# Weight split in a hybrid decoder block: the low part by ScalarE and an accumulating DMA instead of a VectorE subtraction

## The chip, the core and the metric

The kernel runs on one core of a Trainium2 chip. The metric is device microseconds (us) of one execution, lower is better. In the profile the engines are PE (TensorE matmul) with PEld (its weight load), DVE (VectorE), ACT (ScalarE), POOL (GpSimd) and SP (SyncE, which here only issues DMAs).

## The reference

One block of a decoder over 512 tokens of width 1024, with 16 learned meta tokens put ahead (528 columns in all), everything in float32:

```python
h = concat([meta, x])
h = h + 0.5 * swiglu(rmsnorm(h, ffn1_norm), ffn1_w1, ffn1_w3, ffn1_w2)     # D_FF = 2816
hn = rmsnorm(h, mix_norm)
q, k, v, u, g_attn, g_ssm = split(hn @ w_in)
attn = sliding_window_attention(q, k, v, attn_sinks)   # 16 query heads, 4 key heads of 64, window 128
y = gelu(s5_ssm(u, ...))                               # complex diagonal state space layer, 32 groups of 16 channels
ssm = (y @ ssm_glu_a) * sigmoid(y @ ssm_glu_b)
h = h + (sigmoid(g_attn) * attn + sigmoid(g_ssm) * ssm) @ w_out
h = h + 0.5 * swiglu(rmsnorm(h, ffn2_norm), ffn2_w1, ffn2_w3, ffn2_w2)
return rmsnorm(h, final_norm)[meta tokens dropped]
```

with `swiglu(h, w1, w3, w2) = (silu(h @ w1) * (h @ w3)) @ w2`.

## The kernel before

Every product with a weight matrix is made from three products in the format float32r: both operands are split into a high part (the value rounded to float32r) and a low part (the value minus its high part), and `hi*hi + hi*lo + lo*hi` is accumulated in PSUM. Activations stand with the model dimension on the partitions, tokens on the free axis, and a weight tile is [128, nk, 128]: nk blocks of 128 rows of the weight matrix and 128 of its columns.

**The weight stream.** The weights are cut into 200 pieces, in the order in which they are used. `load_raw` (L146) loads one raw tile by a DMA of SP, of mostly 256 columns, so two pieces; two raw buffers are there. `prep_piece` (L160) makes one piece from its raw tile: ScalarE copies it to the tile `whi` (L173, a rounding to float32r), and VectorE subtracts, `wlo = raw - whi` (L174). `whi` and `wlo` have three buffers each. When the last piece of a raw tile is made, the next raw load is issued. The last 8 pieces go to the columns of two larger tiles of their own (`tails`, seen as `hgh` and `hgl`), and so wait for no buffer.

**The units.** A unit is one output block of 128 rows. It takes one piece (`take`, L183), runs 3 * nk matmuls (twice as many, of 264 columns, where the 528 columns are in use; the order for each block k is hi*hi, hi*lo, lo*hi, L234), and is evacuated by VectorE and ScalarE. `step` (L192) emits the matmuls of unit i, then prepares a piece, then emits the evacuation of unit i. Since three pieces exist before unit 2, the piece made behind the matmuls of unit i is that of unit i+2, and its buffers come free when unit i-1 has ended. Every engine runs its instructions in the order in which they are emitted (the schedule is written out by hand), and the framework adds the waits on semaphores.

**The stages**, with the units of each: the first SwiGLU (44 up units with `p` L238, 32 down units at L412, in chunks of 4, 6, 6 and 6 blocks of 128); projections u, k, v and the first of q (10 units), with the state space layer between their matmuls; the mixed stage, 30 units (`MIX`, L25: q, gates, GLU), with the attention of 16 blocks emitted at 11 cuts in each unit, where `prep_piece` is at cut 8 (`CUT`, L41); the output projection (8 units), whose residual `hT` comes back from DRAM by two DMAs of POOL (L1315); the second SwiGLU (44 up units, 24 down units at L414); and the last chunk's down projection by halves of the tokens (16 units at L1372) with the final norm.

**POOL's own work** stands in POOL's one queue: the parameters of the state space layer during the first SwiGLU (`ssm_params`, L472: one chunk at the middle of each unit, L852), the sums of squares for the norms (`sqs`, L835 and L837), and in the mixed stage the normalised probabilities `E` (L1168), the masked meta probabilities `m4` (L1200) and the low part of the queries `qs` (L1130). DMAs issued from POOL are L479 to L496, L666, L869 and L1315.

Of the kernel before, what the change touches and what calls it, by code (L numbers as in the profile page):

```python
# [10 lines left out]
AF = mybir.ActivationFunctionType  # L11
ALU = mybir.AluOpType
# [48 lines left out]
def fr(ap):  # L61
    return ap.bitcast(F32)
# [3 lines left out]
def hybrid_block_kernel(  # L66
# [30 lines left out]
    V, S, G, PE, SY = nc.vector, nc.scalar, nc.gpsimd, nc.tensor, nc.sync  # L97
# [18 lines left out]

# [1 line left out]
    ident = const.tile([128, 128], F32, name="ident")  # L118
    ones = const.tile([128, 128], F32, name="ones")
# [6 lines left out]

# [1 line left out]
    raws = []  # L128
# [31 lines left out]
    def prep_piece():  # L160
        i = nxt["piece"]
        if i >= len(pieces):
            return
        nxt["piece"] += 1
        r, sl, last, dest = pieces[i]
        src = raw_tiles[r][:, :, sl]
        nk = src.shape[1]
        if dest is None:
            hi = w_p.tile([128, nk, 128], F32R, tag="whi", name="whi")
            lo = w_p.tile([128, nk, 128], F32R, tag="wlo", name="wlo")  # L170
        else:
            hi, lo = tails[0][:, dest], tails[1][:, dest]
        S.activation(out=hi, in_=src, func=AF.Copy)  # L173
        V.tensor_tensor(out=lo, in0=src, in1=fr(hi), op=ALU.subtract)  # L174
        wtiles[i] = (hi, lo)
        if last:
            del raw_tiles[r]
            load_raw()

    state = {"unit": 0}  # L180
# [20 lines left out]
    def step2(ua, ub, mids=()):  # L201
        """Two units of which the last tile of operands comes late: it goes last in both."""
        a, b = ua[0](*take(), None), ub[0](*take(), None)
        next(a)
        for m in mids:
            m()
        prep_piece()
        next(b)
        for g in (a, b):
            for _ in g:  # L210
                pass
        ua[1]()
        prep_piece()
        ub[1]()
# [8 lines left out]
    def accumulate(seq, emit, mids):  # L223
        """One accumulation group; the callables in mids go out between its matmuls."""
        cuts = {len(seq) * (j + 1) // (len(mids) + 1): m for j, m in enumerate(mids)}
        for n, args in enumerate(seq):
            if n in cuts:
                cuts[n]()
            emit(*args, n == 0, n == len(seq) - 1)
# [26 lines left out]

# [1 line left out]
    def ffn_plan(w1, w3, w2, chunks, head=0, tail=False):  # L258
# [43 lines left out]

# [1 line left out]
    def new_hg(cols=COLS, p=hg_p):  # L304
# [44 lines left out]

# [1 line left out]
    def ffn_units(hg, hT, n528, mm_ps, g_p, t_p, chunks, last_hook=None, first_mm=None, tail=False):  # L351
        """The units of one half-residual SwiGLU, hT += 0.5 * its output; with tail, the last chunk's
        down projection is left out and its operands are returned."""
        w = HALF if n528 else 256
# [96 lines left out]

# [1 line left out]
    persist = ExitStack()  # L453
# [18 lines left out]
    def ssm_params(ps_p):  # L472
# [113 lines left out]
        V.tensor_copy(dT, ps[:16, 256:288])  # L586
        # the even groups' rows stay on the lower partitions, the odd ones' on the upper
        for i, (dst, q) in enumerate(((c8[:, 0, :], 2), (c8[:, 1, :], 3), (m8, 4))):
# [106 lines left out]

# [1 line left out]
    G.memset(ones, 1.0)  # L697
# [34 lines left out]
    S.activation(out=rcol[:, 0:1], in_=mhalf[:, 0:1], func=AF.Silu)  # L732
    # the tensor engine's clock rises while the first loads are under way
    ps = ax_ps.tile([128, 512], F32, tag="ax", name="ps_w")
# [26 lines left out]
    def x_in(h, d):  # L761
        """Block columns d of token half h: the transpose, then the two parts one and two blocks later."""
        if d < ND:
            x_t(h, d)
        if 0 <= d - 1 < ND:
            x_hi(h, d - 1)
        if 0 <= d - 2 < ND:
            x_lo(h, d - 2)
# [8 lines left out]
    def first_mm(p, hi, lo, mids):  # L777
        """The first two units take the first half of the tokens first, while the second is brought in."""
        firsts.append((p, hi, lo))
# [86 lines left out]

# [1 line left out]
    hd = tc.dram_tile([128, ND, COLS], F32, name="h_keep")  # L868
# [28 lines left out]
    def ev_u(b):  # L897
        """Step-major u: [channel, (step, chunk)], the two chunks of meta tokens first; by way of DRAM
        it comes back as [(7 - step, channel of the group), (group, chunk)]."""
        def f(p):  # L900
            t = s_p.tile([128, T, NCH], F32, tag="uT", name="uT", bufs=2)

            def steps(v, n):
                return v.rearrange("p h (k s) -> p h k s", s=T) if n else v
            for c0, c1, o in ((0, 256, t[:, :, 2:NCH].rearrange("p s (h k) -> p h k s", h=2)),
                              (256, 264, t[:, :, 0:2].rearrange("p s h -> p h s"))):
                V.tensor_tensor(out=o, in0=steps(p[:, :, c0:c1], c0 == 0), in1=steps(rbv[:, :, c0:c1], c0 == 0), op=ALU.mult)
            SY.dma_start(out=ud[b], in_=t)
        return f
# [146 lines left out]

# [1 line left out]
    ps1.close()  # L1058
# [25 lines left out]
    vmeta(0)  # L1084
    # masks, with the sign that the negated scores need
    for t, m0, p0 in ((mA, 0, 16), (mC, 128, 0)):
# [4 lines left out]
                        pattern=[[-1, 128]], channel_multiplier=1)  # L1091
    # hm[p, h]: 1 where row p of the stacked meta probabilities belongs to head h
    V.tensor_reduce(out=hm, in_=ident.rearrange("p (l h k) -> p h l k", l=2, h=4), axis=mybir.AxisListType.XY, op=ALU.add)
# [77 lines left out]
    def s2(n, c, kb):  # L1171
        """One block of keys: the probabilities' transpose."""
        E, _, tiles = att[n][:3]
# [133 lines left out]

# [1 line left out]
    at.close()  # L1309
# [50 lines left out]

    # the last chunk's down projection by halves of the tokens, each half's norm behind the products
    ps5 = ExitStack()
# [114 lines left out]
```

## Time and profile before

| | |
|---|---|
| Median of the timed runs | 1161.17 us (two runs, 1161.1 and 1161.25) |
| Span of the profiled execution, first to last instruction | 1160.7 us |
| Busy: PE / PEld | 1141.6 us (98%) / 1016.8 us (88%) |
| Busy: DVE / ACT / POOL | 632.1 us (54%) / 410.4 us (35%) / 361.5 us (31%) |
| DMA traffic | 108.42 MB, 93 GB/s on average |

The span leaves out what lies around the instructions: the timed runs are 0.4 to 0.6 us longer. A matmul's end is modelled and matmuls overlap, so the duration of one (0.28 to 0.39 us) is more than the distance from one to the next. A row of the profile with "<-" names output and input tiles; a row that ends in "idle before <-releaser" says how long the engine sat idle and what ended that. The chain of work that ended last is followed back from the last instruction.

### The profile page before, as it was taken

What the parts mean: (1) busy time and instruction counts of PE and PEld (TensorE: products, weight loads), DVE (VectorE), ACT (ScalarE), POOL (GpSimd) and SP (SyncE); (2) the same over time, 40 slices, a digit from 0 to 9 for tenths busy, and PEclk for the clock granted to TensorE, in tenths of its full rate; (3) what the DMA queues carried; (4) which work ended last, traced back from release to release, by engine and by line L of the source; (5) the groups of instructions that cost most, each with busy time, mean ns of one, the idle gap of its engine ahead of it and who ended that gap; (6) DMA issues with size and microseconds to landing.
All of it is one profiled execution on the core that took longest, in us unless ns stands there. A gap on an engine that the chain in (4) does not pass through costs nothing.

```text
span 1160.7 us, 17253 instructions
## 1 busy us (share of the span) xinstructions
PE 1141.6 (98%) x7022; PEld 1016.8 (88%) x7022; DVE 632.1 (54%) x956; ACT 410.4 (35%) x719; POOL 361.5 (31%) x488
## 2 busy tenths in 40 slices
PE   9999999999999999999999999999999999999997
PEld 7999999999999999987778778878888888888887
DVE  5446653645444363767776777564544444444454
ACT  5322232232222242446565464353322222232234
POOL 1966662543685030425454331021000000000003
PEclk7999999999999999999999999999999999999999
DMA  5533233322423246121122222432333223323221
GB/s 158 115 96 109 73 92 94 91 84 83 110 74 101 69 144 191 48 73 60 51 73 73 73 68 79 145 109 73 108 109 110 73 82 103 112 86 117 84 73 73
DMA packets 105582, 108.42 MB, mean 93 GB/s; under 512 B 7504, under 2 KB 101968, under 8 KB 105376
## 3 DMA queue, kind: packets, MB, share of 16 engines
q1 hardware_dynamic: 103104, 100.74, 27.8%
q0 software_dynamic: 2352, 6.52, 2.2%
q8 instruction: 55, 0.90, 0.3%
q14 instruction: 23, 0.19, 0.1%
q10 hardware_dynamic: 48, 0.07, 0.0%
HBM read 100.80 MB, written 5.34 MB: 91 GB/s over the span
## 4 chain that ended last, share of the span: by engine, by line
PE 88%; DVE 4%; ACT 3%; POOL 2%; issue 2%; DMA 1%; POOLq 0%; DVEq 0%; SPq 0%; ACTq 0%
PE p L238 58%; PE p L412 11%; PE p L414 8%; PE p L798 2%; PE p L1372 1%; DMA hT<-h_keep 1%; ACT E L1157 1%; POOL m L1200 1%; POOL E L1168 1%; PE psK L656 1%; PE psY L992 1%; DVE wlo L174 1%; PE ps_x L744 1%; PE psY L993 1%; PE psS L943 1%
## 5 line engine op out<-in xcount | busy, mean ns | idle before, releaser
L238 PE MATMUL p<-hgh,whi 128*128 128x264 f32 (+1 forms) x1408 | 403.4, 333 | 0.1
L238 PE MATMUL p<-hgl,whi 128*128 128x264 f32 (+1 forms) x1408 | 402.4, 332 | 0.0
L238 PE MATMUL p<-hgh,wlo 128*128 128x264 f32 (+1 forms) x1408 | 400.9, 331 | 0.5 <-DVE wlo L174 0.5
L174 DVE TENSOR_TENSOR wlo<-raw,whi 128x1024 fp32r<-128x1024 f32 (+2 forms) x192 | 254.0, 1323 | 104.5 <-ACT whi L173 102.2
L238 PEld LDWEIGHTS p<-hgh,whi 128*128 128x128 f32 x1408 | 238.5, 188 | 26.0 <-issue 1.5
L238 PEld LDWEIGHTS p<-hgh,wlo 128*128 128x128 f32 x1408 | 238.2, 188 | 24.6 <-DVE wlo L174 1.0
L238 PEld LDWEIGHTS p<-hgl,whi 128*128 128x128 f32 x1408 | 238.4, 188 | 22.4
L173 ACT ACTIVATE whi<-raw 128x1024 fp32r<-128x1024 f32 (+2 forms) x192 | 187.5, 979 | 133.1 <-PE p L414 72.2
L1388 POOL TENSOR_TENSOR acc<-acc,zq 128x256 f32<-128x256 f32 x12 | 8.9, 738 | 349.8 <-ACT zq L1381 349.7
L384 ACT ACTIVATE t<-t 128x528 f32<-128x528 f32 (+1 forms) x44 | 28.1, 639 | 164.3 <-DVE t L383 164.3
L394 ACT ACTIVATE gh<-t 128x528 fp32r<-128x528 f32 (+1 forms) x44 | 28.1, 639 | 159.2 <-DVE t L393 159.2
L432 DVE SCALAR_TENSOR_TENSOR hT<-p,hT 128x528 f32<-128x528 f32 (+1 forms) x56 | 39.1, 698 | 82.8 <-PE p L414 52.2
L412 PE MATMUL p<-gh,whi 128*128 128x264 f32 x352 | 72.8, 288 | 0.7 <-DVE hT L432 0.5
L412 PE MATMUL p<-gl,whi 128*128 128x264 f32 x352 | 71.5, 284 | 0.0
L412 PE MATMUL p<-gh,wlo 128*128 128x264 f32 x352 | 71.4, 284 | 0.0
L383 DVE TENSOR_TENSOR t<-p,r_bc 128x528 f32<-128x528 f32 (+1 forms) x44 | 30.7, 698 | 70.4 <-PE p L238 67.3
L393 DVE TENSOR_TENSOR t<-p,t 128x528 f32<-128x528 f32 (+1 forms) x44 | 30.7, 698 | 63.8 <-PE p L238 63.5
L412 PEld LDWEIGHTS p<-gh,whi 128*128 128x128 f32 x352 | 54.4, 188 | 2.3 <-issue 1.2
L414 PE MATMUL p<-gh,whi 128*128 128x512 f32 x144 | 56.0, 389 | 0.0
L414 PE MATMUL p<-gl,whi 128*128 128x512 f32 x144 | 56.0, 389 | 0.0
L414 PE MATMUL p<-gh,wlo 128*128 128x512 f32 x144 | 56.0, 389 | 0.0
L412 PEld LDWEIGHTS p<-gl,whi 128*128 128x128 f32 x352 | 54.6, 188 | 0.0
(322 smaller groups left out, 1516.1 us busy)
## 6 DMA issues: line engine op xcount, KB each, us to landing
raw<-in_ffn_w_dram SPq DMA_DIRECT2D x42, 1024.0 KB, 5.4
raw<-in_ffn_w_dram SPq DMA_DIRECT2D x24, 768.0 KB, 4.3
raw<-in_w_in_dram SPq DMA_DIRECT2D x16, 1024.0 KB, 5.5
raw<-in_ffn_w_dram SPq DMA_DIRECT2D x12, 512.0 KB, 3.5
raw<-in_w_out_dram SPq DMA_DIRECT2D x4, 1024.0 KB, 8.7
h_keep<-hT POOLq DMA_DIRECT2D x1, 2112.0 KB, 7.3
raw<-in_ssm_glu_a_dram SPq DMA_DIRECT2D x4, 512.0 KB, 3.6
raw<-in_ssm_glu_b_dram SPq DMA_DIRECT2D x4, 512.0 KB, 4.6
```

The costliest lines, as they stand in the source:

```text
L173: S.activation(out=hi, in_=src, func=AF.Copy)
L174: V.tensor_tensor(out=lo, in0=src, in1=fr(hi), op=ALU.subtract)
L238: PE.matmul(out=o, lhsT=w[:, k0 + k, :], rhs=sl(r, k), start=start, stop=stop)
L383: V.tensor_tensor(out=t1, in0=cell[1], in1=rb(), op=ALU.mult)
L384: S.activation(out=t1, in_=t1, func=AF.Silu)
L393: V.tensor_tensor(out=t3, in0=cell[3], in1=cell["t1"], op=ALU.mult)
L394: S.activation(out=gh, in_=t3, func=AF.Copy)
L412: PE.matmul(out=p[:, h, :HALF], lhsT=wt[:, k, :], rhs=gs[k][c][:, h, :], start=start, stop=stop)
L414: PE.matmul(out=p, lhsT=wt[:, k, :], rhs=gs[k][c].rearrange("p h c -> p (h c)"), start=start, stop=stop)
L432: V.scalar_tensor_tensor(out=hv(hT, d), in0=cell["p"], scalar=0.5, in1=hv(hT, d), op0=ALU.mult, op1=ALU.add)
L656: PE.matmul(out=ps[:16, 128 * i:128 * i + 128], lhsT=BB[:, 0, g, :], rhs=Qt[:, g, 0:T, :].rearrange("p t c -> p (t c)"), start=True, stop= ...
L798: PE.matmul(out=p[:, h, :HALF], lhsT=w[:, k, :], rhs=r[:, k, h * HALF:(h + 1) * HALF], start=(n == 0), stop=(n == 3 * ND - 1))
```

## The change

The subtraction on VectorE goes. ScalarE writes the negated high part into the `lo` tile, and a DMA from POOL reads the same columns of the weight matrix from DRAM a second time and adds them to what the tile holds. A raw tile that has two sources (GLU) takes two such DMAs for a piece. Beside this, comments and docstrings are dropped, which gives no instruction.

```diff
         S.activation(out=hi, in_=src, func=AF.Copy)
-        V.tensor_tensor(out=lo, in0=src, in1=fr(hi), op=ALU.subtract)
+
+        S.activation(out=lo, in_=fr(hi), func=AF.Copy, scale=-1.0)
+        k0 = 0
+        for s in raws[r][2]:
+            n = s.shape[1]
+            G.dma_start(out=lo[:, k0:k0 + n, :], in_=s[:, :, sl], accum_op=ALU.add)
+            k0 += n
         wtiles[i] = (hi, lo)
         if last:
             del raw_tiles[r]
             load_raw()
```

`S` is ScalarE, `V` VectorE, `G` GpSimd. `s[:, :, sl]` takes 128 columns of float32 of each row of the weight matrix, 512 bytes in one piece, nk rows for each of the 128 partitions.

## The prediction

> **What bounds the kernel now.** I read the head of the page first, then the groups, the chain in order of time, the DMA issues, and short stretches of the timeline.
>
> ```profile
> span 1160.7 us, 17253 instructions
> PE 1141.6 (98%) x7022; PEld 1016.8 (88%) x7022; DVE 632.1 (54%) x956; ACT 410.4 (35%) x719; POOL 361.5 (31%) x488
> ...
> PE 88%; DVE 4%; ACT 3%; POOL 2%; issue 2%; DMA 1%; POOLq 0%; DVEq 0%; SPq 0%; ACTq 0%
> ...
> L238 PE MATMUL p<-hgh,wlo 128*128 128x264 f32 (+1 forms) x1408 | 400.9, 331 | 0.5 <-DVE wlo L174 0.5
> L174 DVE TENSOR_TENSOR wlo<-raw,whi 128x1024 fp32r<-128x1024 f32 (+2 forms) x192 | 254.0, 1323 | 104.5 <-ACT whi L173 102.2
> ...
> L173 ACT ACTIVATE whi<-raw 128x1024 fp32r<-128x1024 f32 (+2 forms) x192 | 187.5, 979 | 133.1 <-PE p L414 72.2
> ```
>
> TensorE is busy 98% of the span and makes 88% of the chain. The matmuls that read `wlo` waited 0.5 us for it in the whole run. So the 254.0 us of VectorE that the change takes away lie beside matmuls, and the 19 us in which PE is idle bound any gain: 1.6%, under the 2% that a measurement of this kernel can tell from no change. What can move the time is how late the low part becomes ready. For that the length of a unit counts, from the chain:
>
> ```profile
> 91.27 3.12 PE p L412 x24
> ...
> 155.27 5.87 PE p L238 x48
> ...
> 301.17 4.41 PE p L412 x36
> ...
> 797.68 54.44 PE p L238 x240
> 852.12 32.64 PE p L414 x144
> ```
>
> An up unit takes 5.87 us in the first SwiGLU and 54.44 / 10 = 5.44 in the second; a down unit of six blocks 4.41 and 32.64 / 8 = 4.08, one of four blocks 3.1. The mixed stage, 30 units:
>
> ```profile
> 512.00:718.00 206.00, 198.05 (x977) 160.28 (x976) 154.03 (x350) 118.87 (x284) 87.65 (x57) 1.00 0.21 67
> ```
>
> That is 6.87 us a unit.
>
> **The change part by part.** Removed: 200 subtractions, of no price on PE but for the waits above and a few places named below. Added on ScalarE: a second copy as long as the first, 0.98 us on average, 200 of them, 196 us more on an engine that is busy 410.4. In the mixed stage ScalarE goes from 118.9 to about 150 of 206 us while VectorE loses 1.3 a unit; I count these against each other, at nothing, covered by matmuls; without that cover it is 30 times 1 us at most. Added on POOL: 208 DMA issues (two of half the size for each of the 8 GLU pieces). Added for DRAM: another 100 MB in rows of 512 bytes. The price is T, from the issue to the landing of an accumulating DMA of 512 KB, and no row shows one. The nearest rows:
>
> ```profile
> raw<-in_ffn_w_dram SPq DMA_DIRECT2D x42, 1024.0 KB, 5.4
> ...
> raw<-in_ssm_glu_a_dram SPq DMA_DIRECT2D x4, 512.0 KB, 3.6
> ...
> are<-in_ssm_a_re_dram POOLq DMA_DIRECT2D x1, 8.0 KB, 1.9
> ...
> q1 hardware_dynamic: 103104, 100.74, 27.8%
> q0 software_dynamic: 2352, 6.52, 2.2%
> ...
> DMA to landing us min/median/max: 7.6/9.3/11.0
> ...
> 740.99 0.99 POOL L1315 DMA_DIRECT2D hT<-h_keep  x1 [21.24 <-PE p L238]
> ```
>
> The lowest end is a plain 512 KB, 3.6 us. The highest: POOL's queue q0 took 0.022 * 16 * 1160.7 / 2352 = 174 ns a packet; 1024 rows on 16 engines at one packet a row are 64 * 0.174 = 11.1, with 1.9 of a tiny POOL DMA 13.0 us. Nearest in kind are the two loads of `hT` (the 7.6/9.3/11.0 row): issued by POOL, 128 partitions of 8 rows as here, 1 KB a row, and an accumulation has to bring 512 bytes from DRAM and 512 from the tile for each row. I take 7.6, the one that landed first, and 11.0 where two raw loads of 1 MB are under way. POOL's issue, 0.99 us, is in it.
>
> The Trainium skill, "DMA: Bandwidth & Descriptors", section "Anatomy of one DMA", fits a POOL DMA as 2.0 us plus its bytes at 436 per ns. That would make 3.2 us here, and the sum below would be that of the first rival; for the 1 MB of `hT` it gives 4.4, and the trace, with other transfers beside it, has 7.6. Against the change speaks "Collectives: The Full Stack", section "The bandwidth ceiling": an add in the DMA path is slow because it needs two source reads, not because of the add. With twice the bytes the fit gives 4.4 us for our DMA; no run here shows it yet.
>
> Now the lookahead. The piece for unit i+2 is made when unit i-1 ends. In the second SwiGLU:
>
> ```profile
> 1107.84 0.69 DVE L383 TENSOR_TENSOR t<-p,r_bc 128x512 f32<-128x512 f32 x1 [1.87 <-PE p L238]
> 1108.56 0.63 ACT L384 ACTIVATE t<-t 128x512 f32<-128x512 f32 x1 [3.85 <-DVE t L383]
> ...
> 1109.10 1.04 ACT L173 ACTIVATE whi<-raw 128x1024 fp32r<-128x1024 f32 x1
> ...
> 1110.18 1.23 DVE L174 TENSOR_TENSOR wlo<-raw,whi 128x1024 fp32r<-128x1024 f32 x1 [0.25 <-ACT whi L173]
> ```
>
> The unit has ended by 1107.84, the high part is there at 1110.14, and the negated copy would be at 1111.2, 3.4 us after the end. The first use is the third matmul of unit i+2, 2 * 5.44 + 0.47 later than the end. T is hidden up to 10.88 + 0.47 - 3.4 = 7.9 us; the first SwiGLU has 2 * 5.87 + 0.5 - 3.7 = 8.5. Down units have smaller tiles (T of 6.2 for six blocks, 4.75 for four, from 1.9 plus the share of 5.7) and no ScalarE evacuation: 2 * 4.08 + 0.5 - 1.8 = 6.9 and 2 * 3.1 + 0.4 - 1.3 = 5.3. So at 7.6 the steady SwiGLUs lose nothing. But each four up units load two raw tiles of 1 MB together: at 11.0 us some 3 us are missing, at 22 such places; I take half of them, 30 us. With the DVE subtraction none of this mattered, since it ended 3.6 us after the unit.
>
> In the mixed stage the piece is made late:
>
> ```profile
> 608.87 1.06 ACT L173 ACTIVATE whi<-raw 128x1024 fp32r<-128x1024 f32 x1
> ...
> 608.99 0.39 PE L238 MATMUL p<-YH,whi 128*128 128x512 f32 x1
> ...
> 610.29 2.02 POOL L1200 TENSOR_TENSOR m<-ms,hm 128x512 fp32r<-128x512 f32 x1
> ```
>
> Unit i ends at 608.99, where the next one's first matmul stands. The DMA is queued behind `m4` on POOL, to 612.3, 3.3 us later, and only unit i+1 lies ahead of its use. From the first use in unit i, 0.5 us into it, two periods hold 6.4 + 3.3 + T: the period is (9.7 + T) / 2 = 8.65 us against 6.87. For 16 units with attention that is 29 us. A unit without has no `m4`: with cut 8 at 4.1 us of 5.6 and 2.1 of ScalarE, (5.7 + T) / 2 = 6.65, 1.05 too much; half of it for 14 units is 7. Sum 36. What is queued behind a DMA on POOL there are `E`, `m4` and `qs` of the next unit, for which PE's transposes wait; they come a DMA issue (1 us) later, inside the same stall.
>
> Single places:
>
> ```profile
> 10.12 1.22 DVE L174 TENSOR_TENSOR wlo<-raw,whi 128x1024 fp32r<-128x1024 f32 x1 [0.52 <-ACT whi L173]
> ...
> 13.98 0.64 PE L798 MATMUL p<-hgh,wlo 128*128 128x264 f32 x2
> ...
> 742.55 11.04 DMA hT<-h_keep
> ...
> 756.72 1.24 DVE wlo L174
> 758.00 31.12 PE p L238 x136
> ...
> 1132.45 0.88 DVE hgl L174
> 1134.54 1.43 PE p L1372 x12
> ...
> L509 POOL TENSOR_TENSOR mag<-e,x 32x64 f32<-32x64 f32 x1 | 11.1, 11126 | 0.0
> L642 POOL TENSOR_TENSOR Qt<-Qt,tq 128x1152 f32<-128x1152 f32 x4 | 13.4, 3345 | 0.3
> ```
>
> Start: copy, negated copy and DMA end at 10.1 + 1.0 + 7.6 = 18.8 where PE wants the tile at 13.98: 5 us. Output projection: the chain already runs from the `hT` load over `wlo` to PE; 1.24 becomes 1.05 + 7.6, 7 us, and 3 for `hT` loads that share the DMA engines: 10. Tail: `hgl` is in the chain at 1132.45, with tiles of 256 KB; 0.88 becomes 0.6 + 4.75, perhaps twice: 8. POOL in the first SwiGLU: DMA issues stand between chunks of POOL work of 4 to 6 us (two rows of 2.3 to 3.3 like `Qt`) and once behind `mag`, 11.1, within units of 5.87: 10. There the subtraction also no longer slows POOL's work, which I leave at nothing.
>
> Sum: 30 + 36 + 5 + 10 + 8 + 10 = 99 on the profiled 1160.7, which is 0.5 below the median of the runs: about 1260 us. With both ends of T: at 3.6 the mixed period is 6.65, hidden, and start 1, output 4, tail 2 and POOL 4 remain, 11 us: 1172. At 13.0 by lookahead alone, (9.7 + 13) / 2 adds 4.5 * 30 = 134, and in an up unit three periods hold the lag of 3.7 or 3.4, less 0.5, T, and a unit: (9.1 + T) / 3 and (8.4 + T) / 3, so 1.5 and 1.7 more for 44 units each, 140; the down units by the same form 55, and 55 for the rest: 1545.
>
> **The rivals.**
>
> *Hidden, not slower.* The three buffers cover the DMA, and at T below about 4 the mixed stage too. For: 3.6 us for a plain 512 KB, DMA engines 28% busy with raw loads. Against: the `hT` rows, and the place in the mixed stage where 4.1 us is all there is (6.87 + 0.5 - 3.3). It decides from T = 4.1 down; time 1172, about as long as now. Chance 0.13.
>
> *The DMA engines become the bound.* A raw row costs 0.278 * 16 * 1160.7 / 103104 = 50 ns, so for 512 KB of 977-byte packets raw loads take 537 * 0.050 / 16 = 1.68 us of each engine's time, of the 5.44 to 5.87 of an up unit. What is left allows 59 to 65 ns for each of 64 accumulated rows of 512 bytes. Above that no lookahead helps: at 100 ns 512 KB take 8.1 us, and the 180 tiles of this size that the pieces amount to 1455; at the 174 of q0 12.8, 2306. For: q0's row, and that reading, adding and writing back may not overlap. Against: q0's packets are of 2772 bytes on average. My forecast has 50 ns. Chance 0.26, of it 0.12 above 1650.
>
> *POOL becomes the bound.* An accumulating DMA may take longer to issue than 0.99 us; at 4, T grows by 3, which adds 45 in the mixed stage, 30 and 39 in the up units: 1375 us. POOL has 361.5 us of work, so up to 4.1 a piece it is not full; it decides from 1.3 us of issue on, where T passes 7.9. Chance 0.11.
>
> **How the numbers follow.** The forecast, late landings that the buffers cover only in part (1190 to 1340, at 1260), has 0.50. The range goes from 1170, just under the first rival, to 1650, which leaves 0.06 below and 0.12 above. Faster by over 2% (below 1138) would need more than PE's whole idle time: 0.01. Within 2% (to 1184) is the first rival nearly whole: 0.11. Slower 0.88.
>
> **What the profile after would show.** `wlo` as a DMA of POOL with a landing of about 8 us in the DMA issues, more during raw loads; PE idle of some 100 us, with PE p L238 waiting for DMA `wlo`, most in the mixed stage and at single units of the SwiGLUs; the first wait near 14 us of about 5. VectorE 250 us lower, ScalarE near 600. The DMA share is to rise from 0.30 (q1 and q0) to about 0.75. If it is near 1.0 through the steady SwiGLUs, the second rival holds; if POOL's issues are long, the third. If `wlo` lands in 4 us and PE doesn't wait, I am wrong on T.

## The result and the profile after

The changed kernel takes 1360.33 us (two runs, 1360.03 and 1360.63) against 1161.17: ratio 1.1716, 95% interval 1.1682 to 1.175, so 199 us slower where 99 were forecast.

The page of the kernel after, the lines that answer to those of before:

```profile
span 1358.9 us, 17647 instructions
...
PE 1203.6 (89%) x7022; PEld 1056.3 (78%) x7022; DVE 404.3 (30%) x756; ACT 603.5 (44%) x919; POOL 614.4 (45%) x696
...
q0 software_dynamic: 190000, 100.91, 58.3%
q1 hardware_dynamic: 103104, 100.74, 23.5%
...
PE 34%; issue 22%; DMA 18%; POOL 18%; ACT 6%; DVE 2%; POOLq 0%; DVEq 0%; SPq 0%; ACTq 0%
...
L244 PE MATMUL p<-hgh,wlo 128*128 128x264 f32 (+1 forms) x1408 | 415.6, 342 | 78.9 <-DMA wlo<-in_ffn_w_dram 52.0
...
wlo<-in_ffn_w_dram POOLq DMA_DIRECT2D x88, 512.0 KB, 6.6
```

TensorE's share of the chain fell from 88% to 34%; DMA, POOL and "issue" (time for which the profile shows no wait) took its place. The 198.2 us of the span split in two: PE is idle for 1358.9 - 1203.6 = 155.3 us instead of 19.1, which is 136.2 more, and the same 7022 matmuls are busy 62.0 us longer. The granted clock, on average 0.951 after and 0.991 before, accounts for some 41 of these 62, as worked out further below. The matmuls of L244 with `wlo` wait 78.9 us instead of 0.5. VectorE lost 228 us, ScalarE is at 603.5 and the two DMA queues take 82% of the engines' time: these came about as forecast.

The view of line L179, the new DMA (columns: instructions; min/median/max ns of one issue on POOL):

```profile
L179 POOL DMA_DIRECT2D wlo<-in_ffn_w_dram x144: 1321/1550/2697, 11.9 to 1307.6; - x144
...
DMA to landing us min/median/max: 4.5/6.5/14.4
```

To see where the time went, I took from each trace the start of ScalarE's high-part copy of each of the 200 pieces and subtracted the start of the same piece in the trace of before. The table gives the time lost between one piece and another, in us. A piece is copied about two units ahead of its own unit. The last column is the difference at the end of the span. The variants are explained below. All but mix_only ran once; the kernel before took 1157.9 to 1165.1 us in the runs beside them.

```
pieces                0-8   8-24  24-55 55-63 63-78 78-88 88-118 118-126 126-end |  end
stage               start   first SwiGLU ........... w_in  mixed  output  FFN2,tail
after                13.3  28.8  25.6  42.5   7.2  12.5   21.7    7.8    38.3   | 198.1
act_neg_dve_add       3.9  -2.5   0.4  -0.2   3.6   0.7   13.8    0.3     1.8   |  22.3
gate_on_pool          6.3  11.3  -2.0  33.6   2.9   1.4   19.9    1.3     2.7   |  78.0
plain_dma            10.6  20.7   8.4  37.8   1.7  10.3   -3.7    5.8    13.5   | 105.9
params_on_dve        14.0  24.7  17.5  18.9   7.0  12.0   20.1    7.9    38.5   | 160.8
tables_split         13.3  29.6  24.8   9.3   7.0  11.9   21.3    8.4    34.0   | 160.0
mag_split            14.0  19.5  35.1  22.3  24.7  12.4   20.1    7.7    34.6   | 190.7
lo_last               9.2  27.0  23.8  39.6   7.1   5.7   -2.1    6.5    19.0   | 136.1
lo_last_params_dve    9.1  24.2  16.4  13.0   6.0   6.8   -5.4    6.0    19.4   |  96.1
ll_ffn2_half          7.9  28.3  22.4  39.5   7.0   5.6   -7.2    4.3     4.1   | 111.9
ll_plain              6.9  18.4   5.8  35.1   2.5   4.3   -8.2    4.5     6.2   |  76.0
keep_warm            13.8  28.9  22.6  39.8   5.6  11.6   23.5    8.9    32.8   | 188.0
keep_warm_early      13.4  25.1  18.5  41.6   4.7  13.2   18.2    9.2    32.4   | 177.2
lo_last_before       -4.1  -0.2  -0.5  -0.3  -0.2   0.9    1.6    0.4     0.0   |  -1.6
mix_only             -4.4  -0.2  -0.6  -0.3  -0.2   1.6   -4.7    0.4    -0.1   |  -7.8
```

Where an edit doesn't reach a stage, its rows still differ by up to 7 us (38.3, 34.0, 34.6 and 32.4 in the last stage of kernels with the same code there; -2.1 and -7.2 in the mixed stage; 25.6 and 18.5 in pieces 24 to 55 of after and keep_warm_early). Smaller differences of one row carry nothing. More than half of the loss, 104 us, is in pieces 8 to 78, the first SwiGLU without its first eight pieces, and 42.5 of it in only eight pieces. The timeline of POOL and of one ScalarE copy in the kernel after (columns: start, duration):

```profile
98.55 3.97 POOL L179 DMA_DIRECT2D wlo<-in_ffn_w_dram  x3 [0.19 <-issue]
...
390.15 1.06 ACT L175 ACTIVATE wlo<-whi 128x1024 fp32r<-128x1024 f32 x1
...
390.99 1.47 POOL L179 DMA_DIRECT2D wlo<-in_ffn_w_dram  x1 [0.27 <-issue]
...
405.49 1.58 POOL L179 DMA_DIRECT2D wlo<-in_ffn_w_dram  x1 [0.30 <-issue]
...
420.10 1.59 POOL L179 DMA_DIRECT2D wlo<-in_ffn_w_dram  x1 [0.30 <-issue]
```

DMAs for weights are issued 14.5 us apart, in a stage whose units took 4.41 and 5.87 us before, and three stood in a row at 98.55, behind `mag`, which took 11.09 us. The delays add up: the copy that ends at 391.21 is that of piece 57, and its DMA is the one at 420.10, 28.9 us later. For the pieces 55 to 59 this wait in POOL's queue is 13.2, 18.6, 28.9, 30.8 and 12.4 us; where POOL has no long work it is 0.3 to 0.6. What fills POOL between them is in the groups of POOL of the kernel before, a view of which the prediction used two other rows:

```profile
L467 POOL TENSOR_TENSOR pr<-tt,tt 128x4 f32<-128x4 f32 (+5 forms) x28 | 11.0, 392 | 2.2
L469 POOL TENSOR_TENSOR tt<-pi,pr 128x4 f32<-128x4 f32 (+5 forms) x28 | 10.2, 365 | 0.0
L466 POOL TENSOR_TENSOR tt<-pi 128x4 f32<-128x4 f32 (+5 forms) x28 | 9.6, 344 | 0.0
L468 POOL TENSOR_TENSOR tt<-pr,pi 128x4 f32<-128x4 f32 (+5 forms) x28 | 9.3, 332 | 2.2
L470 POOL TENSOR_TENSOR pi<-tt,tt 128x4 f32<-128x4 f32 (+5 forms) x28 | 9.0, 321 | 2.2
L465 POOL TENSOR_TENSOR tt<-pr 128x4 f32<-128x4 f32 (+5 forms) x28 | 8.8, 314 | 1.9
```

These are 168 small operations, 57.9 us in all, the tables of powers of the state space layer. They are emitted as four chunks of 42, one chunk to a unit. Before, nothing of TensorE waited for them. After, the same operations are faster, 43.6 us in all; a chunk takes 12.4 us from its first to its last, and with the DMA's issue and four small operations ahead of the chunk this makes the 14.5 us. Each chunk stands in the queue ahead of a weight's DMA. Windows of the kernel after show what PE does around them, and the stretch from the last mixed units through most of the second SwiGLU (columns: stretch, length, then busy us and instructions of PE, PEld, DVE, ACT and POOL, the granted clock, the DMA share, GB/s):

```profile
36.00:190.00 154.00, 127.62 (x938) 124.41 (x938) 36.74 (x55) 52.51 (x69) 104.55 (x128) 0.90 0.75 132
...
380.00:460.00 80.00, 50.49 (x333) 49.66 (x332) 7.79 (x11) 16.96 (x18) 52.43 (x181) 0.77 0.51 86
392.00:398.00 6.00, 1.51 (x7) 1.51 (x8) 0.00 (x0) 0.00 (x0) 4.98 (x26) 0.57 0.53 66
404.00:410.00 6.00, 0.00 (x0) 0.00 (x0) 0.00 (x0) 0.00 (x1) 4.96 (x22) 0.71 0.95 224
410.00:416.00 6.00, 3.76 (x17) 3.76 (x18) 0.00 (x0) 0.00 (x0) 4.95 (x20) 0.50 0.31 39
...
860.00:1290.00 430.00, 395.47 (x1672) 319.01 (x1672) 97.09 (x146) 189.02 (x225) 129.97 (x89) 0.97 0.97 176
```

In 392 to 398 POOL works at its tables, PE does 1.51 us and VectorE nothing. In 404 to 410, the DMA issued at 405.49 is on its way, beside a raw load issued at 402.94 (share 0.95), and PE does nothing. In 410 to 416 PE runs at half its clock. In the second SwiGLU it is another resource that is full: the DMA engines, at a share of 0.97.

### The profile page after: what moved, and what is told of

Read it like the earlier page. It is cut to its first block, busy times and chain, and to the rows that moved or that the text cites. A ratio compares the mean times of both kernels' runs of the same rounds, so it can differ in the third digit from the quotient of the medians.

```text
span 1358.9 us, 17647 instructions
## 1 busy us (share of the span) xinstructions
PE 1203.6 (89%) x7022; PEld 1056.3 (78%) x7022; DVE 404.3 (30%) x756; ACT 603.5 (44%) x919; POOL 614.4 (45%) x696
## 4 chain that ended last, share of the span: by engine, by line
PE 34%; issue 22%; DMA 18%; POOL 18%; ACT 6%; DVE 2%; POOLq 0%; DVEq 0%; SPq 0%; ACTq 0%
PE p L244 24%; DMA wlo<-in_ffn_w_dram 9%; POOL wlo L179 7%; DMA wlo<-in_w_in_dram 6%; PE p L418 4%; ACT wlo L175 2%; ACT whi L173 2%; DMA wlo<-in_ssm_glu_b_dram 2%; PE p L1378 1%; PE p L420 1%; DMA wlo<-in_w_out_dram 1%; POOL mag L515 1%; POOL E L1174 1%; ACT E L1163 1%; POOL pr L473 1%
## 5 line engine op out<-in xcount | busy, mean ns | idle before, releaser
L244 PE MATMUL p<-hgh,wlo 128*128 128x264 f32 (+1 forms) x1408 | 415.6, 342 | 78.9 <-DMA wlo<-in_ffn_w_dram 52.0
L179 POOL DMA_DIRECT2D wlo<-in_ffn_w_dram x144 | 223.4, 1574 | 454.8 <-ACT wlo L175 414.2
L244 PE MATMUL p<-hgh,whi 128*128 128x264 f32 (+1 forms) x1408 | 412.3, 340 | 0.1
L244 PE MATMUL p<-hgl,whi 128*128 128x264 f32 (+1 forms) x1408 | 410.4, 338 | 0.0
L244 PEld LDWEIGHTS p<-hgh,wlo 128*128 128x128 f32 x1408 | 246.7, 195 | 114.6 <-DMA wlo<-in_ffn_w_dram 56.8
L244 PEld LDWEIGHTS p<-hgh,whi 128*128 128x128 f32 x1408 | 247.2, 195 | 26.3 <-issue 1.5
L244 PEld LDWEIGHTS p<-hgl,whi 128*128 128x128 f32 x1408 | 245.8, 194 | 23.0
L175 ACT ACTIVATE wlo<-whi 128x1024 fp32r<-128x1024 f32 (+2 forms) x192 | 189.8, 989 | 6.1
L418 PE MATMUL p<-gh,wlo 128*128 128x264 f32 x352 | 79.2, 309 | 38.1 <-DMA wlo<-in_ffn_w_dram 38.0
L418 PEld LDWEIGHTS p<-gh,wlo 128*128 128x128 f32 x352 | 59.9, 207 | 41.9 <-DMA wlo<-in_ffn_w_dram 41.7
L179 POOL DMA_DIRECT2D wlo<-in_w_in_dram x32 | 50.0, 1564 | 74.8 <-ACT wlo L175 74.0
L399 DVE TENSOR_TENSOR t<-p,t 128x528 f32<-128x528 f32 (+1 forms) x44 | 30.8, 699 | 157.3 <-PE p L244 156.9
L420 PE MATMUL p<-gh,wlo 128*128 128x512 f32 x144 | 59.4, 413 | 13.9 <-DMA wlo<-in_ffn_w_dram 13.8
```

Of the source, the lines that this page charges most:

```text
L175: S.activation(out=lo, in_=fr(hi), func=AF.Copy, scale=-1.0)
L179: G.dma_start(out=lo[:, k0:k0 + n, :], in_=s[:, :, sl], accum_op=ALU.add)
L244: PE.matmul(out=o, lhsT=w[:, k0 + k, :], rhs=sl(r, k), start=start, stop=stop)
L399: V.tensor_tensor(out=t3, in0=cell[3], in1=cell["t1"], op=ALU.mult)
L418: PE.matmul(out=p[:, h, :HALF], lhsT=wt[:, k, :], rhs=gs[k][c][:, h, :], start=start, stop=stop)
L420: PE.matmul(out=p, lhsT=wt[:, k, :], rhs=gs[k][c].rearrange("p h c -> p (h c)"), start=start, stop=stop)
```

## The experiments

**ScalarE's second copy without the DMA.** Before, with the negated copy written by ScalarE and the raw tile added to it by VectorE:

```diff
-        V.tensor_tensor(out=lo, in0=src, in1=fr(hi), op=ALU.subtract)
+        S.activation(out=lo, in_=fr(hi), func=AF.Copy, scale=-1.0)
+        V.tensor_tensor(out=lo, in0=src, in1=fr(lo), op=ALU.add)
```

> ScalarE writes the negated high part as in the changed kernel, but VectorE adds the raw tile to it (no accumulating DMA). Theory P (the loss comes from the DMA's place in POOL's queue) and theory D (it comes from the time the DMA takes to land) both say the extra ScalarE copy costs nothing: 1161 to 1168 us. Were the second copy itself the cause, it would be above 1180.

Measured 1184.78 us against 1160.70, so 24 us slower, which neither theory had. The table puts 13.8 of it into the mixed stage. The waits of this kernel there (us in total, times, longest):

```profile
PE ps_s L1153 <- DVE mn L1156: 10.8, 8, 3.5
...
PE ps_tm L1196 <- DVE mn L1156: 5.4, 5, 1.8
```

TensorE's attention waits for VectorE (before, these two waits were 1.7 and 1.6 us), whose addition follows two copies in place of one: VectorE's wait for ScalarE's copies in this stage is 27.2 us instead of 2.9. The copy is thus not free there, though the kernel after doesn't pay it in the same way, since its VectorE has no addition; lo_last below keeps all the copies and loses nothing in the mixed stage. In the SwiGLUs it costs next to nothing.

**POOL's queue without a DMA.** Before, with one operation on a single column put into POOL's queue where the DMA would stand, and VectorE's subtraction waiting for it (the factor is zero):

```diff
-        V.tensor_tensor(out=lo, in0=src, in1=fr(hi), op=ALU.subtract)
+        f = flag[:, i % 4:i % 4 + 1]
+        G.tensor_scalar(out=f, in0=fr(hi)[:, 0, 0:1], scalar1=0.0, scalar2=None, op0=ALU.mult)
+        V.scalar_tensor_tensor(out=lo, in0=src, scalar=f, in1=fr(hi), op0=ALU.add, op1=ALU.subtract)
```

> The kernel before, but VectorE's subtraction takes a scalar (zero) that a one-column instruction of POOL makes from the high part, at the place where the changed kernel issues the DMA: the wait on POOL's queue without a DMA. Theory P: the first SwiGLU loses time behind POOL's long chunks (11.1 us of mag, about 17 us for each part of the tables), less than the changed kernel since 1.3 us follow the gate and not 6.6: 1180 to 1215, with stalls at the same pieces and a lower granted clock. Theory D: 1161 to 1168.

Measured 1240.52 us against 1160.70: 80 us slower, more than expected, and no byte of DMA was added. The waits and the POOL timeline of this kernel:

```profile
DVE wlo L177 <- POOL flag L176: 263.0, 162, 12.0
```

```profile
PE p L415 <- DVE hT L435: 13.2, 5, 6.7
PE p L241 <- DVE hT L435: 13.2, 3, 7.2
```

```profile
337.31 0.21 POOL L176 TENSOR_SCALAR flag<-whi 128x1 f32<-128x1 f32 x1
...
350.91 0.21 POOL L176 TENSOR_SCALAR flag<-whi 128x1 f32<-128x1 f32 x1
```

An operation of 0.21 us appears every 13.6 us, once per chunk of table work, and 33.6 us are lost in pieces 55 to 63, against 42.5 in the kernel after. So a step that has to pass through POOL's queue can cost that much there without any DMA. The way to TensorE is another one, though: here VectorE itself stands in the wait, with its evacuations behind it in its queue. TensorE waits for these, 26.4 us in the two rows with `hT` and 10.8 for `t` of L386, and for `wlo` only 0.4. The run shows the queue, and not what a late low part alone costs. The 19.9 in the mixed stage come by the same way: TensorE's attention waits there 19.5 us for VectorE's `mn`.

**The parameters on VectorE.** After, with the products of the tables and of `LR`, and `Qt`, `tq`, `Pb`, `tm` and `BB`, moved from POOL to VectorE; `mag` stays (two of the lines):

```diff
-                cmul(G, pr[:, js, n + 1:n + 1 + w], pi[:, js, n + 1:n + 1 + w], ...
+                cmul(V, pr[:, js, n + 1:n + 1 + w], pi[:, js, n + 1:n + 1 + w], ...
-            G.tensor_tensor(out=Qt[:, gsl], in0=lam(LR, b, T + 1), ...
+            V.tensor_tensor(out=Qt[:, gsl], in0=lam(LR, b, T + 1), ...
```

> The changed kernel with the large and the many small tensor operations of the S5 parameters (Qt, Pb, tables) on VectorE instead of POOL; the accumulating DMAs are the same. Theory P: the loss of the first SwiGLU (some 100 us) falls to under 40, 1270 to 1305 in all. Theory D: 1345 to 1365, as the landings stay.

1323.36 us: 37 less than after, short of the expected gain. Pieces 55 to 63 go from 42.5 to 18.9 and 24 to 55 from 25.6 to 17.5; the first 24 pieces hardly move.

**The same work on POOL in smaller chunks.** After, with the four table chunks spread over four units each:

```diff
+                if n in (4, 16, 64):
+                    yield
```

> The changed kernel, with each of the four chunks of table work on POOL (about 17 us) cut into four, which go out in four units; the same POOL instructions and DMAs. Theory P (a DMA waits in POOL's queue behind a chunk longer than a unit): the 42 us lost at pieces 55 to 63 fall to under 15, 1322 to 1340 in all, and the half-clock time falls too. Theory D: 1350 to 1365.

1322.56 us against 1360.33. No operation is added or taken away, and pieces 55 to 63 fall from 42.5 to 9.3; other stages stay within 5 us. The wait of a DMA in POOL's queue is 7.7 us at most in this kernel, where it was 30.8. It is the length of the chunk ahead of a DMA that cost there, not POOL's load. This is the cleanest run of the study.

**`mag` in four parts.** After, with the power of 11.1 us done on 16 columns at a time, one part to a unit:

```diff
-        pexp(tl("mag"), tl("x1"), tl("cor"), e32)
+        mag, x1, cor = tl("mag"), tl("x1"), tl("cor")
+        for c in range(0, NST, 16):
+            G.tensor_tensor(out=mag[:, c:c + 16], in0=e32[:, c:c + 16], in1=x1[:, c:c + 16], op=ALU.pow)
+            yield
+        G.tensor_scalar(out=cor, in0=x1, scalar1=E32_REL, scalar2=1.0, op0=ALU.mult, op1=ALU.add)
+        G.tensor_tensor(out=mag, in0=mag, in1=cor, op=ALU.mult)
```

> The changed kernel with the one power operation of 11.1 us on POOL (mag) cut into four of 16 columns, which go out in four units. Theory P: the 7.4 us stall of the unit behind it falls under 3 us and the loss at pieces 8 to 24 from 29 to about 20, 1346 to 1353 in all. Theory D: 1357 to 1363.

1353.21 us, 7 less. Pieces 8 to 24 gain 9.3, but the four new yields move every later chunk by four units: 42.5 becomes 22.3 in pieces 55 to 63 and 7.2 becomes 24.7 in 63 to 78, while pieces 24 to 55 lose 9.5 more. The loss follows the chunks, which again names them; the gain at `mag` itself is the size of what rows of unchanged stages scatter and stays unproven in the total.

**The DMA without the accumulation.** After, with the same transfers and issues, but overwriting. The subtraction is thereby left out and the low part is the whole weight, so only the time is of use:

```diff
-            G.dma_start(out=lo[:, k0:k0 + n, :], in_=s[:, :, sl], accum_op=ALU.add)
+            G.dma_start(out=lo[:, k0:k0 + n, :], in_=s[:, :, sl])
```

> The changed kernel without the accumulation: the same DMAs of POOL overwrite wlo with the raw columns (the low part of the weights is left out and replaced by the whole weight, the time alone is of use). If the accumulation's second read and its write-back make the landing, it falls from 6.6 to under 5 us, the DMA share from 0.82 to about 0.6, and the time by 40 or more, to 1280 to 1320. If issue, queue and small rows make it, it stays above 6 us and the time above 1340.

1268.46 us: the accumulation itself is worth 92 of the 199 us, and 107 remain for the other parts: the copy, the way through POOL's queue and a plain flight. The page of this kernel, and the view of its line L179:

```profile
q0 software_dynamic: 190000, 100.91, 49.2%
...
wlo<-in_ffn_w_dram POOLq DMA_DIRECT2D x88, 512.0 KB, 4.8
```

```profile
L179 POOL DMA_DIRECT2D wlo<-in_ffn_w_dram x144: 750/876/993, 12.3 to 1217.9; - x144
```

An accumulating issue takes 1550 ns of POOL where a plain one takes 876, the landing 6.6 us instead of 4.8, and a packet of q0 0.583 * 16 * 1358.9 / 190000 = 66.7 ns instead of 0.492 * 16 * 1266.7 / 190000 = 52.5. Pieces 55 to 63 lose 37.8 all the same: the queue's part doesn't depend on the kind of DMA.

**The low products last.** After, and as a control before, with all products of `whi` ahead of those of `wlo` in the units that go through `mm3` (up units, projections, GLU), which gives the DMA almost two thirds of a unit more there. Down units have an order of their own, which stays:

```diff
-            seq += [(hi, rhi, k), (hi, rlo, k), (lo, rhi, k)]
+            seq += [(hi, rhi, k), (hi, rlo, k)]
+        seq += [(lo, rhi, k) for k in range(nk)]
```

> The changed kernel, but in every unit that goes through mm3 the products with the low part of the weights come last, so that the first use of wlo is about 3.7 us later. Theory D: what is late by the 6.6 us landing is then in time, the mixed stage, the output projection and the second SwiGLU lose under 20 us together instead of 80, about 1260 to 1290. Theory P: those stages gain as well, but the first SwiGLU still loses 60 or more; 1270 to 1310.

> Control: the kernel before (VectorE subtraction) with the products of the low part of the weights last. PE waits for nothing that this moves, so both theories say 1157 to 1163; the mixed stage, 2.1 us shorter than before in the changed kernel with this order, is as before or shorter by as much if the order itself is what helped there.

After: 1298.61 us, 62 less; before: 1160.98 against 1161.58, no difference. The mixed stage goes from 21.7 to -2.1, w_in from 12.5 to 5.7, the last column from 38.3 to 19.0. Pieces 8 to 63 keep 90.4 of their 96.9. TensorE's waits between 60 and 400 us in this kernel, with L419 in the down units and L245 in the up units, say why:

```profile
PE p L419 <- DMA wlo<-in_ffn_w_dram: 38.6, 15, 8.3
PE p L245 <- DMA wlo<-in_ffn_w_dram: 8.6, 5, 3.5
```

Most of them are in down units, which the edit doesn't touch; and behind the tables a wait of up to 30 us in POOL's queue is too long for a later first use to cover. In pieces 24 to 54 the queue is not the cause: in the kernel after, 21 of these 31 DMAs go out within 0.65 us of their copy, and PE's waits, up to 2.6 us each and mostly in down units, end with landings. With plain DMAs the loss of pieces 24 to 55 fell from 25.6 to 8.4. The total lies in the range of theory P and 9 us above that of theory D, so the places have to speak.

**Both remedies.** lo_last with the parameters on VectorE:

> The changed kernel with both: low products last in the units of mm3 and the S5 parameters on VectorE. The two losses lie at different places, so the gains (62 and 37 us) add: 1255 to 1270, with a clock above 0.97. If both removed the same stalls, it is 1290 or more.

1258.61 us: 40 less than lo_last, where the parameters alone had given 37. The two losses are separate and add up. 97 us remain.

**What is left in the second SwiGLU.** lo_last with the odd pieces of 124 to 191 made by VectorE's subtraction again, and lo_last with plain DMAs:

```diff
+        if 124 <= i < 192 and i % 2:
+            V.tensor_tensor(out=lo, in0=src, in1=fr(hi), op=ALU.subtract)
+        else:
             S.activation(out=lo, in_=fr(hi), func=AF.Copy, scale=-1.0)
            ... (the DMAs, as in the change)
```

> lo_last (1298.6) with every second piece of the second SwiGLU (pieces 124 to 191, odd) made by the VectorE subtraction as before the change; the even ones keep copy and accumulating DMA. Theory 'DMA engines full': in lo_last the second SwiGLU's windows have a DMA share of 1.00 at 182 GB/s, and a unit there brings 1.05 MB in 5.44 us, 193 GB/s. Without half of the additions the share falls to about 0.75 and the stage's loss against before from 19 to at most 5 us: 1279 to 1286 us. Theory 'each landing is late for its own unit': the 34 pieces that are left lose as much each as now, so 9 to 10 us stay: 1288 to 1291.

> lo_last with the second DMA not accumulating; it leaves out the subtraction, so the low part is the whole weight. All copies, issues and places in the queues stay. Theory 'DMA engines full': plain packets took 52.5 ns against 66.7, so a unit of the second SwiGLU needs 1.68 + 64 * 0.0525 = 5.0 us of each engine's 5.44; share near 0.92, the stage's loss falls from 19 to at most 5; with the 15 to 25 us that plain_dma gained on the first stages 1250 to 1265 us. Theory 'each landing is late for its own unit': landings are 1.8 us shorter (4.8 against 6.6), which lo_last's later first use of the low part had mostly covered already; 10 to 19 stay in the second SwiGLU: 1262 to 1275.

1274.45 and 1238.57 us, both below what either theory gave; of the first, 5.1 us come from the mixed stage, which the edit doesn't touch, and the second gained more in pieces 8 to 55 than expected (26.6). In the stage itself 19.0 become 4.1 and 6.2, near the 5 that the theory of full DMA engines gives at most and below the 9 to 10 of the other; with rows that scatter by up to 7 us this alone decides little. Windows of lo_last, ll_ffn2_half and ll_plain in the second SwiGLU:

```profile
900.00:1090.00 190.00, 182.16 (x799) 148.17 (x797) 44.54 (x67) 86.65 (x102) 58.40 (x40) 1.00 1.00 180
```

```profile
890.00:1200.00 310.00, 308.07 (x1361) 254.31 (x1360) 105.80 (x138) 113.52 (x136) 50.40 (x34) 1.00 0.69 144
```

```profile
860.00:1200.00 340.00, 334.54 (x1472) 275.70 (x1471) 77.21 (x115) 155.74 (x183) 60.78 (x71) 1.00 0.89 189
```

lo_last has a share of 1.00 at 180 GB/s, where a unit wants 1.05 MB in 5.44 us, 193 GB/s, and PE is busy 96% of the time. With a quarter of the bytes gone, or with cheaper packets, the share falls to 0.69 and 0.89, PE is busy 99 and 98%, and the loss is gone but for a few us. A rival stays open: from piece 124 on, PE waits 13.2 us for `wlo` in lo_last, and 11.9 of them are in down units, where the first use is as early as before. Both edits also take landings away or shorten them, so full engines and landings late for an early first use are not told apart there.

**The clock.** After, with small matmuls on a constant tile put in before the first product that waits, for four units (55 to 58), or, 12 to 26 of them, for five early ones (3, 6, 10, 14 and 20):

```diff
+            if n == 2 and state["unit"] - 1 in (55, 56, 57, 58):
+                ps = ax_ps.tile([128, 512], F32, tag="ax", name="ps_w")
+                for _ in range(24):
+                    PE.matmul(out=ps[:, 0:128], lhsT=ones, rhs=ones, start=True, stop=True)
```

> The changed kernel with 24 small matmuls on constants (about 6 us at the full clock) put ahead of the first product with wlo in the four units 55 to 58, which stalled 6.2 to 9.7 us behind the tables on POOL; they fill the stall and compute nothing. Theory C (a stall of some us halves the clock of the matmuls behind it, a cost beside the stall): the half-clock time around there goes, and the kernel gets 8 to 14 us faster, 1346 to 1353. If the clock is lowered by something else (the DMA traffic, the mean load), it is 1358 to 1366.

> As keep_warm, but in units 3, 6, 10, 14 and 20, with 12 to 26 small matmuls (3 to 6.5 us at the full clock), a little under each of their stalls of 3.3 to 7.4 us; POOL has only one long chunk there (mag). Theory C, with the clock's cost on the path: the pieces 3 to 24 lose 8 to 14 us less than the changed kernel's 35, 1346 to 1353 in all. If POOL or the landing sets the pace and the slower matmuls are hidden beside them, as keep_warm's own place suggests (2.7 us), it is 0 to 4 us less, 1355 to 1361.

1350.54 and 1339.76 us. Windows of the two kernels:

```profile
380.00:460.00 80.00, 71.21 (x564) 70.64 (x563) 9.21 (x13) 19.64 (x21) 51.60 (x172) 0.93 0.57 96
```

```profile
36.00:190.00 154.00, 143.75 (x1142) 140.18 (x1142) 36.84 (x55) 53.18 (x71) 104.73 (x128) 0.98 0.78 135
```

The granted clock rises from 0.77 to 0.93 in the one stretch and from 0.90 to 0.98 in the other, so it was the pauses of PE that had lowered it. On the path it gives little: 2.7 us at pieces 55 to 63, where POOL's queue sets the pace, and 3.6 up to piece 24 in the early kernel, neither above the scatter of the rows. The rest of the 10 and 21 us that the totals are lower lies in stages that the edits don't touch. What the low clock costs in the whole run is not settled by these two; the time that PE's work lost by it, 41 us, is worked out below.

**Where the change pays.** Before with the order of lo_last, and copy and accumulating DMA for the pieces 86 to 115 only, those of the mixed stage:

> The accumulating DMA only for the 30 pieces of the mixed stage, VectorE's subtraction for all others, and the low products last in mm3. The mixed stage, which is bound by chains over VectorE, ScalarE and POOL, was 2 to 5 us shorter than before in the variants with the low products last: 1155 to 1160 us, the fastest of all. If those gains hung on what came before the stage, it is 1160 to 1166.

1157.34 us (1154.68 to 1159.68) against 1160.58: ratio 0.9967, interval 0.9956 to 0.9978. It beats the kernel before, the faster of the two, by a third of a per cent. Windows of the mixed stage, of mix_only and of the control lo_last_before:

```profile
505.00:720.00 215.00, 212.50 (x1050) 173.71 (x1049) 118.78 (x331) 154.67 (x321) 127.11 (x101) 1.00 0.80 142
```

```profile
505.00:720.00 215.00, 207.19 (x1014) 167.18 (x1013) 155.62 (x351) 120.50 (x287) 89.40 (x57) 0.99 0.21 67
```

VectorE is relieved of 37 us in the stage in which act_neg_dve_add showed TensorE's attention waiting for it, and the 215 us of PE hold 36 matmuls more. That this relief makes the gain fits the rows; no other run tests it. The -4.4 in the first column of mix_only is not the change's: the control has -4.1 there, and both ran their first 36 us at the full clock, where the profile of the kernel before has 0.76.

## Why the prediction was half right

The direction held and the range held the time; the sum was half of what came. By stage, with half of the 30 us for raw bursts counted to each SwiGLU, forecast and loss are: start 5 and 13.3, first SwiGLU 25 and 104, w_in 0 and 12.5, mixed 36 and 21.7, output projection 10 and 7.8, second SwiGLU and tail 23 and 38.3.

- **T, the landing.** Taken as 7.6 us, measured 6.6 for tiles of 512 KB (4.5 to 14.4 over all tiles). The first wait, forecast at 5 us near 14, is 3.9 us; two more among the first eight pieces, 6.3 and 3.3 us at pieces 3 and 6, had no term. The issue was taken from the `hT` load, 0.99, and is 1.55. The Trainium skill, "Collectives: The Full Stack", section "The bandwidth ceiling", which lays the slowness of ReduceScatter's add on its two source reads, has the direction: against plain copies, packets cost 1.27 times as much, not twice.
- **The term that failed: "POOL in the first SwiGLU", 10 us.** It was priced from `Qt` rows of 2.3 to 3.3 and `mag`. With half of the raw bursts, 25 us stood against the 104 that pieces 8 to 78 lost, 79 of the 99 us that were missing. The largest part are the four table chunks, which no row over 0.4 us betrays: they show only when the six groups are summed and divided by the four chunks. Behind them a DMA stood up to 30.8 us in the queue, and 42.5 us were lost in eight pieces. tables_split shows that it was the chunks' length: it brought 33.2 of them back. gate_on_pool lost 33.6 at the same place with the queue alone, by a different way to TensorE.
- **A second step that failed: the steady first SwiGLU at nothing but for raw bursts.** The lookahead of its down units was taken to cover T. Pieces 24 to 55 lost 25.6 us; PE's waits for landings there are 18.4 us, 13.0 of them in down units. With plain DMAs the loss was 8.4. How much of this is raw bursts was not tried.
- **Mixed stage: 36 forecast, 21.7 lost.** The mechanism, a late piece used early in the next unit, held: with the low products last nothing is lost there. Two of its terms were too high: T is 6.7 us there in the median, and a DMA goes out 0.4 us behind its copy, not 1.3 (611.0 to 612.3 behind `m4`). With both, the prediction's own form gives periods of 7.75 and 6.2 us, so about 18 us in all, an estimate near the 21.7.
- **Output projection: 10 forecast, 7.8 lost.** Held.
- **Second SwiGLU and tail: 15 and 8 forecast, 38.3 lost.** Here the second rival fits. It named 59 to 65 ns a row as its point; 66.7 were measured, and the DMA share is 0.97. About 19 of the 38 us were landings late for the first use of up units (38.3 to 19.0 in lo_last). Some 13 to 15 of the rest went with fewer bytes or cheaper packets (19.0 to 4.1 and 6.2), which full engines explain, but late landings in down units have a part in it that no run separates. In the first SwiGLU the share was 0.75 and 0.51 in the stretches shown, so there the rival doesn't decide.
- **w_in: nothing forecast, 12.5 lost.** The state space layer's work stood between the matmuls; lo_last takes half. One wait of 6.2 us, for piece 79, came with a landing of 11.4 us; why that landing was so long was not tried.
- **The second ScalarE copy at nothing** held in the SwiGLUs; in the mixed stage the same copy cost 13.8 where VectorE had to wait for it, inside the 30 that the prediction named for the case without cover.
- **The clock had no term.** PE's matmuls are busy 62.0 us longer. In the trace's record of the granted clock it is either full or half, half in 24 stretches after, of 3.4, 6.8 or 10.2 us but for the last, and in 2 before, one of 17.1 us at the start and one at the end. PE is busy for 99.8 us inside them after and for 17.1 before; half of that is lost, 49.9 and 8.5, so about 41 of the 62 us are the clock's. Where the other 21 come from is open. Ahead of each of the 24, PE was idle for 1.9 to 3.4 of the last 3.4 us. The Trainium skill, "TensorE: Matmul & The Clock Gate", section "Part 1: The HAM clock gate", has this rule: the clock is either half or full, and falls to half after an idle window of about 3.4 us. The trace agrees with the steps, though 1.9 idle us in the window were enough here, and the prediction had not read it as a price on every stall.
- **The other rivals.** "Hidden" fell. The bound by POOL's issue time gave 1375, near the time that came, by another mechanism: the issue did pass its 1.3 us, but T with it is 6.6 and not 7.9, and what makes the wait is other work in the queue.

Of the 97 us that lo_last_params_dve still loses, 63 are in the first 63 pieces (9.1, 24.2, 16.4 and 13.0); `mag`, the down units with their early first use, the plain way through the queue and the half clock all lie there, and their shares stay open.

## What to carry to other kernels

A step that is moved to a DMA of another engine is moved into that engine's queue: sum up the longest run of work between two places where the issue can stand, not the longest single instruction, since chunks of 42 operations of 0.3 us held DMAs up by 12 to 31 us. Look at what each stall of TensorE does to the clock of the matmuls behind it, even if it was worth little on the path where it was tried here, and compare the bytes of a unit with what the DMA engines moved when their share was 1.00. Take such a change only into the stage where the relieved engine is waited for, with the first use of the result as late as the accumulation order allows: here that turned a loss of 17% into a gain of 0.3%.

## What the runs showed of the hardware

- An accumulating DMA of 512 KB in rows of 512 bytes took 6.6 us in the median to land and 1.55 us of POOL to issue, a plain one 4.8 and 0.88; packets took 66.7 and 52.5 ns.
- The 16 DMA engines, at a share of 1.00, moved 180 GB/s with this mix of raw loads and accumulations (lo_last, 900 to 1090 us).
- The granted clock of TensorE fell to half, in steps of 3.4 us, after stretches of 3.4 us in which PE was idle for 1.9 us or more.
- Some small matmuls on constant data held the granted clock through the pauses (0.77 to 0.93), for 2.7 us on the path at that place.
